# Half of the low halves of a kernel's last weights made by an adding DMA in the place of a VectorE subtraction

## The chip, the cores and the metric

The kernel runs on 1 core of one Trainium2 chip. The metric is device time in microseconds (us), the median of several runs. Before the change it is 1040.36 us, median of 3 runs (1040.05 to 1041.47).

## The reference, cut to what matters

Three transformer blocks follow one another over 256 tokens of 1024 features: a forgetting attention with a SwiGLU feed-forward, a retention with a SwiGLU feed-forward and a last norm, and a hybrid of differential and sparse attention with a gated feed-forward. All is float32. The part that the change reaches is the last block:

```
h = rms_norm(x, attn_pre_norm)
mix = hybrid_mixer(h, ...)            # projections, two kinds of heads, concat @ w_out
x = x + rms_norm(mix, attn_post_norm)
h = rms_norm(x, ffn_pre_norm)
f = (silu(h @ w_gate) * (h @ w_up)) @ w_down      # w_gate, w_up: 1024 x 2816; w_down: 2816 x 1024
x = x + rms_norm(f, ffn_post_norm)
```

## The kernel before, in words

Every product with a weight matrix is made in three matmuls of a reduced-precision float type (fp32r): each operand is split in a high half, the operand rounded to fp32r, and a low half, the operand minus its high half; high x high, high x low and low x high are summed in PSUM (mm3, L228 to L230; mm_wide at L243 and L244 does the same in two matmuls with both halves of the activations side by side).

The weights are read once, in granules of 128 x 1024 floats, 512 KB (some are smaller). The plan of all granules is a list in the order of use, 342 long. `gran` makes one: SP loads it into one of 4 raw buffers (L218), ACT copies it to wh, rounding it (L221), and DVE subtracts wh from raw into wl (L222). wh and wl have 6 buffers each. `take` hands the next granule to a caller and makes those ahead, up to 6 from the one that is taken, so that a granule's buffers are filled again as soon as PE is done with the granule 6 before it. `self.made` counts the granules made.

The order of the instructions on each engine is set by a scheduler when the program is built, from the order of the code and its own costs; each engine then runs its queue in order.

The last block: the hybrid's projections and heads, from some 735 us on. While the heads run (DVE and ACT do the softmax, the sparse heads first and then the differential ones), PE fills in with the projection of the differential heads from hyb_w (12 granules, `parts`) and then with w_out (8 granules). diff_norm squares the heads' outputs on ACT (don, da), POOL raises to -1/2 (dr), DVE scales (don). The handover follows: post_prep squares the sum on ACT (sq), POOL makes the reciprocal root (nr, L325), DVE updates x (xg) and scales it (pg), PE turns it (tr), and ACT and DVE split it again (xt, L249 and L250), for the first 128 tokens and then for the others. The last feed-forward (ffn with out set) takes 8 granules of 2 x 512 columns for gate and up of the first 512 columns (xs: all four gate granules for the first token tile, then for the second), then 36 granules of gate and up in pairs (ws_wide), the dense stretch, and 22 rows of w_down (out_proj), of which the last four are used bank after bank at the end.

Of the kernel before, what the change touches and what calls it, by code (L numbers as in the profile page):

```python
# [10 lines left out]
F32 = mybir.dt.float32  # L11
F32R = mybir.dt.float32r
AF = mybir.ActivationFunctionType
OP = mybir.AluOpType
# [124 lines left out]
class Net:  # L139
    def __init__(self, ctx, tc, ins):  # L140
        self.ctx, self.tc, self.nc = ctx, tc, tc.nc
        self.ins = ins
        self.c0, self.c1, self.c2 = (ins[f"const_{i}"] for i in range(3))
        nc = self.nc
        P = lambda name, bufs, **kw: ctx.enter_context(tc.tile_pool(name=name, bufs=bufs, **kw))
        self.cst = P("cst", 1)
        self.wp = P("wp", 1)
        self.sm = P("sm", 4)
        self.scr = P("scr", 2)
        self.ps = P("ps", 1, space=PSUM)  # L150
        cst = self.cst
        c0 = cst.tile([128, 808], F32, name="c0")
        self.c0t = c0
        self.ident = c0[:, 0:128]
        self.upper = c0[:, 128:256]
        self.ones = c0[:, 256:384]
        self.mask3 = c0[:, 384:768]
        self.sum8 = c0[0:16, 768:776]
        self.sum32 = c0[0:64, 776:808]
        self.xg = cst.tile([128, 48 + 8 * S], F32, name="xg")  # L160
        self.gT = self.xg[:, 0:48].rearrange("p (i k) -> p i k", i=6)
        self.XR = self.xg[:, 48:48 + 8 * S].rearrange("p (k s) -> p k s", k=8)
        self.gfg = cst.tile([128, 8], F32, name="gfg")
        self.XT = cst.tile([128, 8, 2, S], F32R, name="xt")
        self.XH, self.XL = self.XT[:, :, 0, :], self.XT[:, :, 1, :]
        self.mhalf = cst.tile([128, 8], F32, name="mhalf")
        nc.gpsimd.memset(self.mhalf, -0.5)
        self.r = [None, None]
        self.scale = None
        self.squares = []  # L170
        self.queue, self.ready, self.taken, self.made = [], [], 0, 0

    def phase_pool(self, ctx, name):
# [40 lines left out]
    def gran(self, src, nk):  # L214
        nc = self.nc
        n = src.shape[-1]
        w = self.wp.tile([128, n], F32, name="raw", tag="raw", bufs=4)
        nc.sync.dma_start(w, src)  # L218
        H = self.wp.tile([128, n], F32R, name="wh", tag="wh", bufs=WBUFS)
        L = self.wp.tile([128, n], F32R, name="wl", tag="wl", bufs=WBUFS)  # L220
        nc.scalar.activation(H, w, AF.Copy)  # L221
        nc.vector.tensor_sub(L, w, H.bitcast(F32))  # L222
        cut = lambda a: a.rearrange("p (k n) -> p k n", k=nk)
        return cut(H), cut(L)

# [660 lines left out]
    def hybrid(self, gp, gn):  # L886
        nc = self.nc
        ins = self.ins
        TT, STT = nc.vector.tensor_tensor, nc.vector.scalar_tensor_tensor
        with ExitStack() as st:  # L890
# [274 lines left out]
            def out_tiles(i):  # L1165
                OH[i] = p.tile([128, 4, S], F32R, name=f"oh{i}", tag="oT", bufs=4)
                OL[i] = p.tile([128, 4, S], F32R, name=f"ol{i}", tag="oT", bufs=4)
# [3 lines left out]
            def d_evac(i, t, ps):  # L1171
# [6 lines left out]
                else:  # L1178
                    a = p.tile([128, 512], F32, name=f"dv{t}")
                    nc.scalar.activation(a, ps, AF.Copy, scale=rr[t])  # L1180
                    dv.append(a)

            out_tiles(1)
            parts = []
            for i in range(3):
# [215 lines left out]
```

## Time and profile before

| | |
|---|---|
| median of 3 runs | 1040.36 us (1040.05 to 1041.47) |
| the profiled execution | 1041.37 us |
| its span, first to last instruction | 1039.6 us |
| PE, PEld busy | 98%, 84% of the span |
| DVE, ACT, POOL busy | 71%, 55%, 2% |
| mean granted TensorE clock | 0.996 |
| bytes moved | 181.18 MB, mean 174 GB/s |

The profile is of one execution. PE is the matmul engine and PEld its weight load, DVE is VectorE, ACT ScalarE, POOL GpSimd, SP the engine that issues the loads. Busy times of pipelined matmuls overlap, so a busy PE isn't PE at its peak; a wait in brackets behind a row is idle time of that engine just before it, with what ended it. The granted clock is a share of 2.4 GHz. Line numbers (L222) are those of the kernel before.

### The profile page before, as it was taken

What the parts mean: (1) busy time and instruction counts of PE and PEld (TensorE: products, weight loads), DVE (VectorE), ACT (ScalarE), POOL (GpSimd) and SP (SyncE); (2) the same over time, 40 slices, a digit from 0 to 9 for tenths busy, and PEclk for the clock granted to TensorE, in tenths of its full rate; (3) what the DMA queues carried; (4) which work ended last, traced back from release to release, by engine and by line L of the source; (5) the groups of instructions that cost most, each with busy time, mean ns of one, the idle gap of its engine ahead of it and who ended that gap; (6) DMA issues with size and microseconds to landing.
All of it is one profiled execution on the core that took longest, in us unless ns stands there. A gap on an engine that the chain in (4) does not pass through costs nothing.

```text
span 1039.6 us, 15367 instructions
## 1 busy us (share of the span) xinstructions
PE 1022.5 (98%) x5798; PEld 876.8 (84%) x5798; DVE 733.0 (71%) x1243; ACT 568.6 (55%) x914; POOL 19.8 (2%) x30
## 2 busy tenths in 40 slices
PE   7999999999999999999999999999999989999997
PEld 6999888888889889888888888888787668888885
DVE  6855977766777766767777777778887676776643
ACT  6545665665453353355565655556656665566532
POOL 1000000000000000000000000000000010000000
PEclk9999999999999999999999999999989999999999
DMA  8643666556665456456666666655633146566651
GB/s 267 217 146 118 234 184 197 183 179 185 188 201 173 151 162 183 141 171 195 215 211 186 182 188 186 184 174 175 210 104 120 31 154 202 193 183 191 192 172 40
DMA packets 53384, 181.18 MB, mean 174 GB/s; under 512 B 6832, under 2 KB 8368, under 8 KB 53184
## 3 DMA queue, kind: packets, MB, share of 16 engines
q1 hardware_dynamic: 53280, 180.19, 55.5%
q8 instruction: 45, 0.74, 0.3%
q14 instruction: 27, 0.22, 0.1%
q0 software_dynamic: 32, 0.03, 0.0%
HBM read 179.15 MB, written 1.05 MB: 173 GB/s over the span
## 4 chain that ended last, share of the span: by engine, by line
PE 95%; DVE 2%; DMA 1%; ACT 1%; issue 1%; POOL 0%; DVEq 0%; ACTq 0%; POOLq 0%
PE acc L243 23%; PE acc L244 12%; PE s L243 11%; PE acc L228 11%; PE acc L230 11%; PE acc L229 11%; PE s L244 6%; PE o L1154 1%; DVE wl L222 1%; PE o L228 1%; PE o L230 1%; PE o L229 1%; DMA raw<-in_hyb_w_dram 0%; DMA raw<-in_v_w_dram 0%; PE tr L845 0%
## 5 line engine op out<-in xcount | busy, mean ns | idle before, releaser
L222 DVE TENSOR_TENSOR wl<-raw,wh 128x1024 fp32r<-128x1024 f32 (+2 forms) x342 | 406.8, 1192 | 206.7 <-ACT wh L221 206.1
L221 ACT ACTIVATE wh<-raw 128x1024 fp32r<-128x1024 f32 (+2 forms) x342 | 352.7, 1033 | 278.4 <-PE acc L230 64.5
L243 PE MATMUL acc<-xt,wh 128*128 128x512 f32 x496 | 180.7, 397 | 0.0
L243 PE MATMUL s<-xt,wh 128*128 128x512 f32 x496 | 180.6, 397 | 0.0
L244 PE MATMUL acc<-xt,wl 128*128 128x256 f32 x496 | 129.5, 281 | 0.0
L244 PE MATMUL s<-xt,wl 128*128 128x256 f32 x496 | 129.3, 281 | 0.0
L243 PE MATMUL acc<-ht,wh 128*128 128x512 f32 x352 | 122.1, 392 | 0.0
L228 PE MATMUL acc<-wh,xt 128*128 128x512 f32 (+1 forms) x288 | 116.5, 405 | 1.9 <-ACT xt L249 1.8
L230 PE MATMUL acc<-wh,xt 128*128 128x512 f32 (+1 forms) x288 | 114.9, 399 | 1.2 <-DVE xt L250 1.2
L229 PE MATMUL acc<-wl,xt 128*128 128x512 f32 (+1 forms) x288 | 114.4, 397 | 0.0
L243 PEld LDWEIGHTS acc<-xt,wh 128*128 128x128 f32 x496 | 93.3, 188 | 16.8
L243 PEld LDWEIGHTS s<-xt,wh 128*128 128x128 f32 x496 | 93.3, 188 | 16.8
L244 PEld LDWEIGHTS s<-xt,wl 128*128 128x128 f32 x496 | 93.6, 189 | 5.9
L244 PEld LDWEIGHTS acc<-xt,wl 128*128 128x128 f32 x496 | 93.7, 189 | 5.6
L244 PE MATMUL acc<-ht,wl 128*128 128x256 f32 x352 | 96.6, 282 | 0.0
L243 PEld LDWEIGHTS acc<-ht,wh 128*128 128x128 f32 x352 | 65.1, 188 | 13.4
L228 PE MATMUL acc<-xt,wh 128*128 128x256 f32 x256 | 73.2, 286 | 0.0
L230 PE MATMUL acc<-xt,wl 128*128 128x256 f32 x256 | 72.1, 282 | 0.0
L229 PE MATMUL acc<-xt,wh 128*128 128x256 f32 x256 | 72.1, 281 | 0.0
L244 PEld LDWEIGHTS acc<-ht,wl 128*128 128x128 f32 x352 | 66.3, 188 | 1.5
L228 PEld LDWEIGHTS acc<-wh,xt 128*128 128x128 f32 x288 | 55.0, 191 | 14.6 <-ACT xt L249 2.2
L230 PEld LDWEIGHTS acc<-wh,xt 128*128 128x128 f32 x288 | 55.2, 192 | 13.4 <-DVE xt L250 1.6
(350 smaller groups left out, 1510.5 us busy)
## 6 DMA issues: line engine op xcount, KB each, us to landing
raw<-in_ffn_w_dram SPq DMA_DIRECT2D x132, 512.0 KB, 3.7
raw<-in_ret_w_dram SPq DMA_DIRECT2D x48, 512.0 KB, 3.5
raw<-in_ffn_out_dram SPq DMA_DIRECT2D x32, 512.0 KB, 3.7
raw<-in_w_down_dram SPq DMA_DIRECT2D x22, 512.0 KB, 3.6
raw<-in_fox_w_dram SPq DMA_DIRECT2D x20, 512.0 KB, 4.6
raw<-in_hyb_w_dram SPq DMA_DIRECT2D x20, 512.0 KB, 4.1
raw<-in_ret_out_dram SPq DMA_DIRECT2D x16, 512.0 KB, 3.9
raw<-in_ffn_out_dram SPq DMA_DIRECT2D x16, 384.0 KB, 3.5
```

The lines of the kernel that those rows point to most:

```text
L221: nc.scalar.activation(H, w, AF.Copy)
L222: nc.vector.tensor_sub(L, w, H.bitcast(F32))
L228: mm(out, xh, wh, start=first, stop=False, **kw)
L229: mm(out, xh, wl, start=False, stop=False, **kw)
L230: self.last = mm(out, xl, wh, start=False, stop=last, **kw).ins
L243: whole = lambda: mm(ps, H, x, start=first, stop=last).ins
L244: part = lambda: mm(ps[:, 0, :], L, x[:, 0, :], start=False, stop=False).ins
L1154: nc.tensor.matmul(o[hs, t, :], VN[i // 2][:, i % 2, g, :], pt[:, 2 * t + i, :], start=i == 0, stop=i == n - 1)
```

## The change

A flag is set where the hybrid's sparse heads begin. From there on, each granule with an odd number gets its low half in another way: ACT writes the negated high half into wl, and POOL issues a DMA that reads the weights a second time from DRAM and adds them to wl.

```
         H = self.wp.tile([128, n], F32R, name="wh", tag="wh", bufs=WBUFS)
         L = self.wp.tile([128, n], F32R, name="wl", tag="wl", bufs=WBUFS)
         nc.scalar.activation(H, w, AF.Copy)
-        nc.vector.tensor_sub(L, w, H.bitcast(F32))
+        if self.dma_low and self.made % 2:
+            nc.scalar.activation(L, H.bitcast(F32), AF.Copy, scale=-1.0)
+            nc.gpsimd.dma_start(L, src, accum_op=OP.add)
+        else:
+            nc.vector.tensor_sub(L, w, H.bitcast(F32))
...
+            self.dma_low = True
             out_tiles(1)
             parts = []
```

In __init__ the flag is set to False, which moves the lines behind it by one; behind gran they are moved by five and behind the flag by six, so L222 of before is L227 of the change, and its negating copy and DMA are L224 and L225.

The order of the instructions changes with it, from the stretch of the heads on. POOL, from the middle of the program to its end, before (nr are reciprocal roots of norms, xc a buffer that is cleared):

```order
L338 TENSOR_TENSOR nr_5093<-nv,mhalf 128x2
L979 MEMSET xc 128x512 x2
L338 TENSOR_TENSOR nr_6915<-nv,mhalf 128x2
L338 TENSOR_TENSOR nr_6924<-nw,mhalf 128x2
L1243 TENSOR_TENSOR dr<-da,mhalf 128x4 x2
L325 TENSOR_TENSOR nr<-nv,mhalf 128x1 x6
```

And in the change, from the heads on:

```order
L225 DMA wl<-in_hyb_w_dram 128x1024 x4
L225 DMA wl<-in_w_out_dram 128x1024 x3
L1249 TENSOR_TENSOR dr<-da,mhalf 128x4 x2
L225 DMA wl<-in_w_out_dram 128x1024
L225 DMA wl<-in_ffn_w_dram 128x1024
L330 TENSOR_TENSOR nr<-nv,mhalf 128x1 x2
L225 DMA wl<-in_ffn_w_dram 128x1024
L330 TENSOR_TENSOR nr<-nv,mhalf 128x1
L225 DMA wl<-in_ffn_w_dram 128x1024
L330 TENSOR_TENSOR nr<-nv,mhalf 128x1
L225 DMA wl<-in_ffn_w_dram 128x1024 x19
L225 DMA wl<-in_w_down_dram 128x1024 x11
```

The DMAs stand between the small operations of the norms, 41 in all.

DVE at the end of the heads, before (da and don are diff_norm's, ol the low half of its result):

```order
L250 TENSOR_TENSOR ol_8100<-tr,oh_8099 128x512
L222 TENSOR_TENSOR wl<-raw,wh 128x1024 x3
L1241 TENSOR_SCALAR da<-da 128x4
L1245 SCALAR_TENSOR_TENSOR don<-o,dr,subln 128x128 x4
L222 TENSOR_TENSOR wl<-raw,wh 128x1024
```

And in the change:

```order
L255 TENSOR_TENSOR ol_8106<-tr,oh_8105 128x512
L227 TENSOR_TENSOR wl<-raw,wh 128x1024
L1247 TENSOR_SCALAR da<-da 128x4
L1251 SCALAR_TENSOR_TENSOR don<-o,dr,subln 128x128 x4
L227 TENSOR_TENSOR wl<-raw,wh 128x1024
```

Three subtractions ahead of the second da have become one.

DVE a little later, at the end of the handover's first token tile, before (xg and pg are post_prep's, xt the low half of what PE multiplies next):

```order
L495 TENSOR_TENSOR pg<-acc,gain 128x512
L513 SCALAR_TENSOR_TENSOR xg<-pg,nr,xg 128x4x128 x2
L514 TENSOR_TENSOR pg<-xg,gain 128x512 x2
L222 TENSOR_TENSOR wl<-raw,wh 128x1024 x2
L250 TENSOR_TENSOR xt<-tr,xt 128x4x128 x2
```

And in the change (nv takes ACT's squares of x, nf takes POOL's nr):

```order
L500 TENSOR_TENSOR pg<-acc,gain 128x512
L518 SCALAR_TENSOR_TENSOR xg<-pg,nr,xg 128x4x128 x2
L519 TENSOR_TENSOR pg<-xg,gain 128x512 x2
L227 TENSOR_TENSOR wl<-raw,wh 128x1024
L328 SCALAR_TENSOR_TENSOR nv<-na 128x1
L493 TENSOR_SCALAR nf<-nr 128x1
L255 TENSOR_TENSOR xt<-tr,xt 128x4x128 x2
```

One of the two subtractions ahead of xt is gone, and nv and nf have moved in front of xt.

ACT in the handover, from the first token tile's xt to the second's, before (sq are the squares for the norms, sg the gate's activation):

```order
L249 ACTIVATE xt<-tr 128x4x128 x2
L318 ACTIVATE sq,na<-xg 128x512
L221 ACTIVATE wh<-raw 128x1024
L318 ACTIVATE sq,na<-acc 128x512
L221 ACTIVATE wh<-raw 128x1024
L318 ACTIVATE sq,na<-s 128x512
L318 ACTIVATE sq,na<-xg 128x512 x2
L611 ACT_TABLE_LOAD
L611 ACTIVATE sg<-acc,nr 128x512
L249 ACTIVATE xt<-tr 128x4x128 x2
```

And in the change:

```order
L254 ACTIVATE xt<-tr 128x4x128 x2
L323 ACTIVATE sq,na<-acc 128x512
L224 ACTIVATE wl<-wh 128x1024
L323 ACTIVATE sq,na<-s 128x512
L222 ACTIVATE wh<-raw 128x1024 x2
L224 ACTIVATE wl<-wh 128x1024
L323 ACTIVATE sq,na<-xg 128x512 x2
L616 ACT_TABLE_LOAD
L616 ACTIVATE sg<-acc,nr 128x512
L254 ACTIVATE xt<-tr 128x4x128 x2
```

Negated copies (L224) have come in between the squares, and two wh copies and one negated copy stand ahead of the second pair of sq<-xg.

PE between the two groups of 16 matmuls of 16 columns, which make the compressed scores, before (the last two of the first group and the first of the second):

```order
L1081 MATMUL o<-KCH,QS_7168 128x16
L1082 MATMUL o<-KCL,QS_7168 128x16
L1121 MATMUL s<-KTH,QS_7168 128x256
L1122 MATMUL s<-KTL,QS_7168 128x256
L229 MATMUL acc<-wl,xt 128x512
L230 MATMUL acc<-wh,xt 128x512
L228 MATMUL acc<-wh,xt 128x512
L1081 MATMUL o<-KCH,QS_7169 128x16
```

And in the change:

```order
L1086 MATMUL o<-KCH,QS_7168 128x16
L1087 MATMUL o<-KCL,QS_7168 128x16
L234 MATMUL acc<-wl,xt 128x512
L235 MATMUL acc<-wh,xt 128x512
L233 MATMUL acc<-wh,xt 128x512
L234 MATMUL acc<-wl,xt 128x512
L1086 MATMUL o<-KCH,QS_7169 128x16
```

The two scores matmuls of 256 columns have moved ahead of the first group, and one matmul of 512 columns more stands between the groups.

## Rows read from the trace of the kernel before

**Rows 1.** The page: busy us by engine (share of span), and chain by engine.
```profile
PE 1022.5 (98%) x5798; PEld 876.8 (84%) x5798; DVE 733.0 (71%) x1243; ACT 568.6 (55%) x914; POOL 19.8 (2%) x30
...
PE 95%; DVE 2%; DMA 1%; ACT 1%; issue 1%; POOL 0%; DVEq 0%; ACTq 0%; POOLq 0%
```

**Rows 2.** Timeline of PE, 820 to 853: start, us, [idle before].
```profile
831.86 0.50 PE L1251 MATMUL tr<-c,don 128*128 128x128 f32 x2 [0.60 <-DVE don L1245]
...
843.99 0.50 PE L230 MATMUL acc<-wh,xt 128*128 128x512 f32 x1 [1.21 <-DVE xt L250]
...
848.06 0.39 PE L229 MATMUL acc<-wl,xt 128*128 128x512 f32 x1
...
852.00 0.50 PE L228 MATMUL acc<-wh,xt 128*128 128x512 f32 x1 [1.54 <-ACT xt L249]
```

**Rows 3.** Windows: length, each engine's busy us; last clock, DMA share, GB/s.
```profile
880.00:970.00 90.00, 90.00 (x512) 78.30 (x512) 65.00 (x88) 54.68 (x80) 0.00 (x0) 1.00 0.60 187
...
730.00:740.00 10.00, 9.25 (x49) 6.97 (x47) 9.27 (x15) 6.69 (x8) 0.00 (x0) 1.00 0.82 277
728.00:729.00 1.00, 1.00 (x6) 0.82 (x5) 0.10 (x2) 0.87 (x1) 0.00 (x0) 1.00 0.98 401
```

**Rows 4.** Groups of instructions by line, 760 to 1040: busy, mean ns.
```profile
L222 DVE TENSOR_TENSOR wl<-raw,wh 128x1024 fp32r<-128x1024 f32 x77 | 93.8, 1223 | 57.4 <-ACT wh L221 57.3
L221 ACT ACTIVATE wh<-raw 128x1024 fp32r<-128x1024 f32 x76 | 80.2, 1057 | 55.8 <-PE o L230 26.2 <-PE s L243 17.0 <-PE acc L230 9.0
```

**Rows 5.** Timeline of ACT in the dense stretch, 919 to 932.
```profile
919.61 1.06 ACT L221 ACTIVATE wh<-raw 128x1024 fp32r<-128x1024 f32 x1 [0.95 <-PE s L243]
921.10 0.39 ACT L637 ACTIVATE sg<-s 128x256 f32<-128x256 f32 x1 [0.42 <-PE s L243]
921.38 1.05 ACT L221 ACTIVATE wh<-raw 128x1024 fp32r<-128x1024 f32 x1
...
925.26 1.06 ACT L221 ACTIVATE wh<-raw 128x1024 fp32r<-128x1024 f32 x1 [0.95 <-PE s L243]
```

**Rows 6.** DMA issues: count, KB each, us to landing; POOL's issue in ns.
```profile
raw<-in_ffn_w_dram SPq DMA_DIRECT2D x132, 512.0 KB, 3.7
...
f<-in_fox_f_dram POOLq DMA_DIRECT2D x1, 32.0 KB, 3.6
...
L549 POOL DMA_DIRECT2D f<-in_fox_f_dram x1: 708/708/708, 1.3 to 1.3; - x1
```

**Rows 7.** Timeline of SP from 850, and of DVE and PE near the end.
```profile
850.95 96.11 SPq L218 DMA_DIRECT2D raw<-in_ffn_w_dram  x35
950.19 57.87 SPq L218 DMA_DIRECT2D raw<-in_w_down_dram  x22
...
1017.63 1.23 DVE L222 TENSOR_TENSOR wl<-raw,wh 128x1024 fp32r<-128x1024 f32 x1 [1.56 <-ACT wh L221]
...
1024.24 0.40 PE L229 MATMUL acc<-wl,ht 128*128 128x512 f32 x1
```

**Rows 8.** Timeline of DVE, then POOL, in the handover.
```profile
826.48 3.68 DVE L222 TENSOR_TENSOR wl<-raw,wh 128x1024 fp32r<-128x1024 f32 x3 [0.26 <-ACT wh L221]
...
840.98 2.36 DVE L222 TENSOR_TENSOR wl<-raw,wh 128x1024 fp32r<-128x1024 f32 x2
...
844.68 1.46 POOL L325 TENSOR_TENSOR nr<-nv,mhalf 128x1 f32<-128x1 f32 x1 [6.27 <-DVE nv L323]
```

**Rows 9.** Timeline of ACT in the handover.
```profile
843.95 0.59 ACT L318 ACTIVATE sq<-acc 128x512 f32<-128x512 f32 x1
...
847.91 0.63 ACT L318 ACTIVATE sq<-xg 128x512 f32<-128x512 f32 x1 [1.76 <-DVE xg L513]
```

**Rows 10.** Windows of a microsecond where the granted clock falls (columns as in rows 3).
```profile
758.00:759.00 1.00, 1.00 (x10) 1.00 (x9) 0.00 (x0) 0.00 (x0) 0.00 (x0) 0.76 0.83 229
759.00:760.00 1.00, 1.00 (x4) 0.90 (x5) 0.63 (x3) 0.00 (x0) 0.00 (x0) 0.50 0.66 172
...
765.00:766.00 1.00, 1.00 (x8) 0.81 (x7) 0.00 (x0) 0.20 (x1) 0.00 (x0) 0.83 0.06 16
```

More of the change, by code (lines that the diff above doesn't have):

```diff
@@ L170, in __init__ @@
         self.squares = []
+        self.dma_low = False
         self.queue, self.ready, self.taken, self.made = [], [], 0, 0
```

## The prediction

> **What bounds the kernel now.** I read the page's busy table and its chain first: PE is busy 1022.5 of 1039.6 us, DVE 733.0, and 95% of the chain that ended last is PE [rows 1]. So work that moves between DVE, ACT and the DMA engines gains only where PE is seen to wait, and loses wherever an operand of PE comes late. Then the PE timeline of the stretch in which the change begins: its three longest waits stand in the handover from the hybrid to the last feed-forward, 0.60, 1.21 and 1.54 us [rows 2], each behind a chain through DVE, ACT and POOL; from there to the end PE has no idle time of note. Then the windows of the dense stretch: in 880 to 970 PE is busy 90.00 of 90 us, ACT 54.68, and the 16 DMA engines have a share of 0.60 at 187 GB/s [rows 3]. The profiled execution took 1041.37 us for a span of 1039.6 and lies 1.0 above the median of the three runs, 1040.36; I sum against it and take the 1.0 off at the end. About 0.2%, 2.1 us, is what a measurement of this kernel can tell from no change.
>
> **The parts.** The order of POOL lists 41 adding DMAs, 4 + 4 for the hybrid, 22 for gate and up, 11 for down, so the change does what it says and no rival is needed for that.
>
> *DVE* loses 41 subtractions of 1223 ns [rows 4], 50 us. In the dense stretch PE doesn't wait for DVE, so this is worth nothing there; its cover is the lead of six buffers.
>
> *ACT* gains 41 copies of the shape of the wh copy, 1057 ns [rows 4], 43 us. In the dense stretch that is one per pair of granules. A pair lasts 5.65 us (919.61 to 925.26 [rows 5]), so 16 copies add 17 us to 54.68 of 90 and ACT stays below full. The lead holds too: PE ends a pair at about 921.1, ACT makes the second granule's high half from 921.38 [rows 5] and the negated one until about 923.5. PE wants that buffer two pairs and a quarter later, at 921.1 + 11.3 + 1.4 = 933.8. The add has some 10 us from issue to use.
>
> *POOL* issues the adds. The one DMA it issued before, of 128 rows, took 708 ns of it and 3.6 us to landing [rows 6]. 41 of these make 29 us on an engine with nothing else to do in the dense stretch. The nr pows stand behind an issue in POOL's queue, but each such issue follows a copy that ACT makes ahead of the sq that feeds the pow, so it has 0.6 us of sq as cover: nothing, or a tenth or two if the cover goes.
>
> *The adding DMA* has no row. Per granule it moves 512 KB, and it must read its destination beside its source. Below, it costs the DMA engines one plain pass; above, three (two reads and a write in turn). I take two, because a plain pass holds one read and this one holds two. A pass takes 512 KB over the rate of full queues. The rows give 187 GB/s at share 0.60, 277 at 0.82 and 401 at 0.98 [rows 3], which is 312, 338 and 409 per full share: queues that are fuller move more per busy time, so I take the last, 1.31 us a pass; the second gives 1.55. From 850.95 on SP still issues 35 + 22 = 57 plain loads [rows 7], and 30 adds fall in the same time, 117 passes. At 1.31 us they end 153 us later, at 1004; at 1.55, at 1032. Before, the last low half was ready at 1017.63 + 1.23 = 1018.9, and PE first used it at 1024.24 [rows 7]. So by my value the adds are hidden: 0 us. At 1.55 they cost 1032 - 1024 = 8. The Trainium skill (Collectives: The Full Stack, the section on the bandwidth ceiling) says that a DMA that adds emits two read descriptors per chunk on the same ring and so delivers about half the rate of a copy, 32.35 against 62.28 GB/s; by it the sum would be the one above, with two passes, and no row here shows it. It speaks against the change.
>
> *The handover* is the place where I expect a visible difference. A gain: DVE did three subtractions (826.48, 3.68 us) ahead of the second da [rows 8]; now one stands there, and ACT makes the don squares after two wh copies instead of three, so da comes some 1 us earlier and the wait of 0.60 goes, -0.6. No gain: two subtractions at 840.98 held DVE's xt up [rows 8] and one is left, 1.2 us less, but in the new order nv and nf of the first token tile stand ahead of xt too, and nf waits for POOL's nr, which took 1.46 us here [rows 8]. With wl until 842.2, nv, and nr until 843.9, the first half of xt is ready near 844.6, where it let PE go at 843.99 [rows 2]: +0.7, with the gain +0.1. A cost: the fourth granule of gate (the second of the feed-forward that is added) gets its negated half on ACT behind both xt and the first sq of the second token tile. That sq ran at 843.95 [rows 9] for 0.6, so the copy ends near 845.6, and 0.6 earlier with the gain ahead of it, 845.0. A plain load of 512 KB lands 3.7 us after its issue [rows 6], here at 848.7, and with a second pass of 1.31 at 850.0. PE reached this granule's low half at 848.06 [rows 2], now at 848.2: a new wait of 0.5 to 1.8 us. Behind it ACT does two wh and one negated copy, 3.2 us, ahead of the next sq, in the place of one wh and 1.76 us of idle time [rows 9], some 1.3 us later; but the xt that PE waits for at 852.00 also stands behind the gate's sg, which waits for the same late accumulator, so the two delays run side by side and are not summed. The handover gives +0.6 to +1.9; bounds -1.8, if both waits ahead go, and +1.9. I take +1.0, what the plain landing gives and a third of the second pass.
>
> *The clock.* From 758 to 766 PE ran at a granted clock of 0.50, which is 1.2 GHz of 2.4, after 32 matmuls of 16 columns. The loss is 0.24 + 6 x 0.50 + 0.17 = 3.4 us (six full microseconds at 0.50, their neighbours at 0.76 and 0.83 [rows 10]). The new order keeps both groups of 16 with four wide matmuls between them, so I take 0; bounds -3.4 and +3.4 (a second fall).
>
> Sum: 1041.4 + 0 + 1.0 + 0 - 1.0 = about 1041, no change that can be told.
>
> **The rivals.**
>
> *The DMA engines become the bound.* If the queues can't go past the rate of the ten-microsecond window, the adds pile up in the dense stretch and PE waits for wl a little in every pair. It decides from the point at which 57 loads and 30 adds need more than 1024 - 851 = 173 us, a pass of 1.48 us at two passes per add. At 1.55 us it costs 8 us; by the share of the dense stretch itself (0.60 of 5.65 us for two granules, 1.70 a pass) 117 passes end at 1050, +26. Between them +14: 1055 (1046 to 1067). For it: no ten-microsecond window moves more than 277 GB/s [rows 3]. Against: the last row of [rows 3], and 10 us of lead. The Trainium skill (DMA: Bandwidth & Descriptors, Issuing engines are not separate DMA queues) says that DMAs from POOL run on the same 16 engines as those from SP and interleave with them; by that rule the second queue brings no rate of its own, as this rival has it.
>
> *Three passes or more.* 147 passes end at 850.95 + 193 = 1044 or, at 1.55 us, 1079: +20 to +55, some 1080. Nothing in the rows speaks for it but that no row excludes it.
>
> *Faster.* The fourth granule's add is in time and POOL's nr is over before DVE comes to nf, so that the waits of 0.60 and 1.21 go, -1.8; or the clock no longer falls, -3.4; or both, -5.2: about 1037.5, between 1035 and 1038.5. For it: DVE was the engine ahead of two of the three waits. Against: ACT takes what DVE gives, in the same chain.
>
> **How the numbers follow.** Hidden with a handover that is about even: 0.46, 1041 (1038 to 1045, mostly inside the 2.1 us). DMA-bound: 0.28. Three passes: 0.11. Faster: 0.15. Faster by over 0.2% takes 0.14 from the last and 0.09 from the first: 0.23. Slower takes 0.28, 0.11 and 0.10 from the first: 0.49. The rest, 0.28, is no change. The single likeliest case is no change, though the slower ones together hold more; its own range is 1038 to 1045. The range of 8 in 10 goes from 1036 to 1066 and leaves out the third case and the outer ends of the DMA-bound and the faster one.
>
> **What would show it.** In the changed profile the dense stretch should read 280 GB/s or more with PE at 90.00 of 90, ACT near 72, and no PE wait with wl's DMA as releaser; the DMA share tells how many passes an add has (0.9 is one, near 1.0 with a landing of 6 to 8 us is two). At the handover a wait of 0.5 to 2 us on the add of a gate granule, and none of 0.60 ahead of the second don. I am wrong if PE waits for wl in most pairs from 880 on (the first rival), if landings exceed 10 us (the second), or if the clock's fall near 760 is gone (the third).

## The result and the profile after

| | before | after |
|---|---|---|
| median | 1040.36 us (1040.05 to 1041.47) | 1048.2 us (1045.28 to 1050.95, 5 runs) |
| the profiled execution | 1041.37 us | 1046.59 us |
| its span | 1039.6 us | 1044.8 us |
| last matmul's end to the end of the span | 6.4 us | 6.9 us |
| mean granted TensorE clock | 0.996 | 0.996 |

The change is slower: the ratio is 1.0074, with a 95% interval from 1.0062 to 1.0085, or 7.8 us. The profiled execution is one of the shorter; in the three runs above 1048 us the mean granted clock is 0.991 or 0.992 where it is 0.996 here, and 0.004 to 0.005 of 1047 us is 4 to 5 us.

The page of the changed kernel, busy time by engine, the two DMA queues (packets, MB, share of 16 engines), and the chain by engine; the first and last of these lines answer to [rows 1]:

```profile
PE 1023.1 (98%) x5798; PEld 876.5 (84%) x5798; DVE 687.3 (66%) x1202; ACT 606.8 (58%) x955; POOL 53.2 (5%) x71
...
q1 hardware_dynamic: 53280, 180.19, 53.3%
q0 software_dynamic: 5936, 21.53, 11.5%
...
PE 92%; DMA 3%; DVE 2%; issue 1%; ACT 1%; POOL 0%; DVEq 0%; ACTq 0%; POOLq 0%
```

DVE is 45.7 us less busy and ACT 38.2 us more, and a second queue moves 21.5 MB, as the change says. What is new is DMA in the chain. The dense stretch, as in [rows 3], the windows of the changed kernel:

```profile
880.00:970.00 90.00, 90.00 (x513) 78.30 (x512) 47.19 (x73) 67.90 (x96) 13.63 (x16) 1.00 1.02 281
```

PE is busy 90.00 of 90 us as before, while the DMA share rose from 0.60 to 1.02 and the rate from 187 to 281 GB/s. So the loss isn't there. The waits of PE from 734 us on, changed kernel (us in total, times, longest):

```profile
PE acc L234 <- DMA wl<-in_ffn_w_dram: 3.3, 1, 3.3
PE acc L234 <- DMA wl<-in_w_out_dram: 2.3, 1, 2.3
PE acc L234 <- DMA wl<-in_hyb_w_dram: 1.5, 1, 1.5
PE acc L233 <- ACT xt L254: 1.4, 2, 1.1
PE acc L233 <- DVE rm L933: 0.4, 1, 0.4
PE tr L1257 <- DVE don L1251: 0.3, 1, 0.3
```

and the same view of the kernel before:

```profile
PE acc L228 <- ACT xt L249: 1.8, 2, 1.5
PE acc L230 <- DVE xt L250: 1.2, 1, 1.2
PE tr L1251 <- DVE don L1245: 1.2, 2, 0.6
PE tr L965 <- DVE nat L930: 0.6, 2, 0.4
```

The handover's waits, 4.2 us before (1.8 + 1.2 + 1.2), are 1.7 now (1.4 + 0.3), so 2.5 us are gained; three waits for an adding DMA, one each, cost 7.1. That is +4.6 of the 5.2 us between the two spans; 0.5 is the longer tail behind the last matmul. The three in the timeline of PE, each a matmul with the low half of an added granule:

```profile
751.59 0.51 PE L234 MATMUL acc<-wl,xt 128*128 128x512 f32 x1 [1.54 <-DMA wl<-in_hyb_w_dram]
...
833.66 0.50 PE L234 MATMUL acc<-wl,oh 128*128 128x512 f32 x1 [2.26 <-DMA wl<-in_w_out_dram]
...
851.11 0.67 PE L234 MATMUL acc<-wl,xt 128*128 128x512 f32 x1 [3.28 <-DMA wl<-in_ffn_w_dram]
```

The chain of the changed kernel (start, us, what) shows how long each add took from its issue to its landing:

```profile
742.68 8.87 DMA wl<-in_hyb_w_dram
...
827.67 5.95 DMA wl<-in_w_out_dram
...
845.12 5.95 DMA wl<-in_ffn_w_dram
```

By their place in the plan these are granules 261 (the first that is added), 275 (the last of w_out) and 279 (the fourth of gate and up, the one that the prediction looked at). PE wanted them at the start of its row less the wait in brackets, at 750.05, 831.40 and 847.83: they had a lead of 7.4, 3.7 and 2.7 us. In the dense stretch an add lands in 7.4 us (median), and PE waits for none there; the prediction's estimate of its lead was some 10 us.

The clock. The fall at 758 of [rows 10] isn't there in the changed kernel's profile, but two others are, right behind the two longer waits (windows, columns as in [rows 3]):

```profile
834.00:835.00 1.00, 1.00 (x4) 0.84 (x3) 0.00 (x0) 0.51 (x2) 0.00 (x0) 0.60 1.07 287
835.00:836.00 1.00, 1.00 (x4) 0.71 (x4) 0.69 (x1) 0.17 (x2) 0.00 (x0) 0.50 1.00 303
...
852.00:853.00 1.00, 1.00 (x4) 0.80 (x3) 0.00 (x0) 0.00 (x0) 0.00 (x0) 0.50 0.99 385
```

Each costs 1.7 us (for the first 0.40 + 0.50 + 0.50 + 0.31 in its four windows), together the 3.4 us of the fall before. In this one execution the clock therefore adds nothing.

### The profile page after: what moved, and what is told of

The parts are those of the page before. It is cut to its first block, busy times and chain, and to the rows that moved or that the text cites. A ratio compares the mean times of both kernels' runs of the same rounds, so it can differ in the third digit from the quotient of the medians.

```text
span 1044.8 us, 15432 instructions
## 1 busy us (share of the span) xinstructions
PE 1023.1 (98%) x5798; PEld 876.5 (84%) x5798; DVE 687.3 (66%) x1202; ACT 606.8 (58%) x955; POOL 53.2 (5%) x71
## 3 DMA queue, kind: packets, MB, share of 16 engines
HBM read 200.64 MB, written 1.05 MB: 193 GB/s over the span
## 4 chain that ended last, share of the span: by engine, by line
PE 92%; DMA 3%; DVE 2%; issue 1%; ACT 1%; POOL 0%; DVEq 0%; ACTq 0%; POOLq 0%
PE acc L248 23%; PE acc L249 12%; PE s L248 11%; PE acc L234 10%; PE acc L235 10%; PE acc L233 10%; PE s L249 6%; PE o L1159 1%; DMA wl<-in_hyb_w_dram 1%; DVE wl L227 1%; DMA wl<-in_w_out_dram 1%; DMA wl<-in_ffn_w_dram 1%; PE o L233 1%; PE o L235 1%; PE o L234 1%
## 5 line engine op out<-in xcount | busy, mean ns | idle before, releaser
L222 ACT ACTIVATE wh<-raw 128x1024 fp32r<-128x1024 f32 (+2 forms) x342 | 352.7, 1033 | 265.3 <-PE acc L235 65.2
L227 DVE TENSOR_TENSOR wl<-raw,wh 128x1024 fp32r<-128x1024 f32 (+3 forms) x301 | 357.2, 1188 | 216.5 <-ACT wh L222 215.6
L235 PE MATMUL acc<-wh,xt 128*128 128x512 f32 (+1 forms) x288 | 114.4, 398 | 0.0
L235 PE MATMUL acc<-xt,wl 128*128 128x256 f32 x256 | 72.1, 282 | 0.0
L234 PEld LDWEIGHTS acc<-wl,xt 128*128 128x128 f32 x288 | 54.9, 191 | 17.6 <-DMA wl<-in_ffn_w_dram 3.7
L233 PEld LDWEIGHTS acc<-wh,xt 128*128 128x128 f32 x288 | 54.9, 191 | 14.1 <-ACT xt L254 1.8
```

Of the source, the lines that this page charges most:

```text
L233: mm(out, xh, wh, start=first, stop=False, **kw)
L234: mm(out, xh, wl, start=False, stop=False, **kw)
L235: self.last = mm(out, xl, wh, start=False, stop=last, **kw).ins
```

## The experiments

Theory A: the adds are free wherever a granule is made with the full lead of six buffers; the loss is a few adds where the stages change, which land after PE wants them, and the clock that falls behind such waits. Theory B: the second read fills the DMA queues, and this costs in the dense stretch. Theory C: the cost is the new order in heads and handover with ACT's extra copies, not the DMA. All kernels are the changed one with another condition in gran; a granule that isn't added is subtracted on DVE. The ratios are to the kernel before as it was timed beside each group of runs: 1040.38, 1040.13 and 1040.37 us.

### The dense adds alone, and the early ones alone

```
-        if self.dma_low and self.made % 2:
+        if self.dma_low and self.made % 2 and self.made >= 284:
```

> The adds are left in only from granule 284 on, in the dense stretch (29 of 41); the heads and the handover subtract on VectorE as before. Theory A (the loss is three late adds at the changes of stage, and the clock that falls behind such waits; adds with the lead of six buffers are free): 1040.4 us, 1039.5 to 1042, with PE at 90.00 of 90 in 880 to 970, a DMA share near 1.0 there, no wait of PE on an add but some 0.3 us at the very end. Theory B (the second read fills the DMA queues and costs time in the dense stretch): most of the 7.8 us remain, 1045 to 1048. Theory C (the new order of the heads and ScalarE's extra copies there are the cost, not the adds themselves): about 1040, as A.

Measured: 1042.02 us, ratio 1.0015 [1.0006, 1.0023], 1.6 us. The window 880 to 970 has the change's traffic and no loss:

```profile
880.00:970.00 90.00, 90.00 (x512) 78.33 (x511) 47.54 (x72) 67.53 (x97) 13.76 (x16) 1.00 1.00 277
```

PE's waits in the handover are those of the kernel before and none is for an add; the last matmul ends at 1033.22 us, where before it ended at 1033.23. In this profile only the tail is 0.5 us longer. The other microsecond of the 1.6 isn't seen in it. The time lies at the upper edge of A's range, and C expected the same as A here: the run speaks against B alone.

```
-        if self.dma_low and self.made % 2:
+        if self.dma_low and self.made % 2 and self.made < 284:
```

> The adds are left in only up to granule 283 (12 of 41): hybrid, w_out and the first two of the feed-forward, and nothing in the dense stretch changes against the kernel before. Theory A: the whole loss, 1046 to 1049, with the same three waits of PE of about 1.5, 2.3 and 3.3 us and the granted clock falling to 0.50 behind at least one of them. Theory B: about 1040 to 1042, since the dense stretch has its old traffic of 187 GB/s. Theory C: the whole loss, as A.

Measured: 1047.8 us, ratio 1.008 [1.0068, 1.0093], 7.4 us: nearly the whole loss from 12 adds of 41, with no added traffic in the dense stretch. So B falls. The waits of PE:

```profile
PE acc L234 <- DMA wl<-in_w_out_dram: 3.2, 1, 3.2
PE acc L234 <- DMA wl<-in_ffn_w_dram: 2.8, 1, 2.8
PE acc L233 <- ACT xt L254: 1.7, 2, 0.9
```

The same two late adds; the first, of hyb_w, wasn't waited for. Behind the second the clock was below full from 848 to 859, nine whole microseconds of it at 0.50.

### Without the three that PE waited for

```
-        if self.dma_low and self.made % 2:
+        if self.dma_low and self.made % 2 and self.made not in (261, 275, 279):
```

> Three adds of 41 are taken out, those PE waited for: the first (granule 261, hyb_w), the one that stood behind the second dr on GpSimd (275, w_out) and the second of the feed-forward (279); VectorE subtracts there. Theory A: the waits of 1.5, 2.3 and 3.3 us go, 7.1 us, and the handover stays 2.5 us shorter than before: 1037 to 1041, with no wait on an add above 0.5 us, unless the next add in line (263 or 277) is then late itself, which would give 1040 to 1043. Theory B: 1045 or more, since 38 of 41 adds are still there. Theory C: 1044 to 1048, since nearly all of ScalarE's copies and of the new order stay.

Measured: 1043.88 us, ratio 1.003 [1.0018, 1.0042]. The waits on adds are gone, and the time is 4.3 us below the change's, but it is above A's range, and above the 1040 to 1043 for another late add. A new wait stands behind the handover (timeline of PE, then the DVE row it waits for, with the one ahead of it):

```profile
870.29 0.86 PE L623 MATMUL tr<-c,sg 128*128 128x128 f32 x4 [2.66 <-DVE sg L620]
```

```profile
868.40 1.23 DVE L227 TENSOR_TENSOR wl<-raw,wh 128x1024 fp32r<-128x1024 f32 x1 [6.70 <-ACT wh L222]
869.55 1.28 DVE L620 TENSOR_TENSOR sg<-acc,sg 128x512 f32<-128x512 f32 x2
```

The gate's product sg stands behind a subtraction whose high half ACT makes late: by its row that copy waited for a matmul of PE (L235) and began at 867.32. I took this for the queues being full of adds; the last run below shows that this isn't enough. The wait isn't the whole either. In this profile the clock fell three times, near 758, at 843 and behind the wait at 870, and this cost 6.8 us where the kernel before lost 3.4 [rows 10]. A window of the second fall:

```profile
844.00:845.00 1.00, 1.00 (x4) 0.77 (x3) 0.95 (x2) 0.19 (x1) 0.50 (x1) 0.50 0.82 299
```

### What an add costs: two in a pair

```
-        if self.dma_low and self.made % 2:
+        if self.dma_low and self.made >= 284:
```

> Every granule from 284 on gets its low half by an add (58 adds, two per pair of granules in the place of one), none ahead of it; VectorE subtracts no weights there. This prices an add at the DMA engines: a pair lasts 5.65 us and now holds two plain loads and two adds. If an add costs what two plain passes cost (1.31 us each, six passes), a pair takes 7.9 us and the dense stretch and w_down grow by some 60 us, to 1100. If it costs 1.4 plain passes at the lower rate of the old dense stretch (1.70 us a pass), 8.2 us a pair, 1110. If it costs one pass at 1.31, 5.2 us a pair, still hidden: 1040 to 1045. Theory B would have any of the longer ones; theory A says nothing here but that one add per pair fits.

Measured: 1101.93 us, ratio 1.0596 [1.0576, 1.0615], where two passes per add were put at 1100. The two queues in 880 to 970 (packets, MB, share), and the two largest of PE's waits from 850 on:

```profile
q0 software_dynamic: 3386, 12.36, 68.7%
q1 hardware_dynamic: 3387, 12.34, 36.5%
```

```profile
PE acc L249 <- DMA wl<-in_ffn_w_dram: 23.4, 17, 2.9
PE acc L234 <- DMA wl<-in_w_down_dram: 15.2, 19, 1.5
```

Here the queues are the bound, and both carry the same bytes: an add takes 68.7 / 36.5 = 1.88 times the engines of a plain load. (In the dense stretch of the change the queues have 51.8% for 8.39 MB and 49.5% for 16.85 MB, which makes it 2.1.) 12.34 MB are 23.5 loads of 512 KB, and as many adds; 23.5 + 1.88 x 23.6 = 67.9 plain passes in 90 us are 1.33 us a pass. With one add per pair, 2 + 1.88 passes would take 5.15 of 5.65 us: by this estimate the change's dense stretch has half a microsecond per pair to spare, and a second add overruns it.

### ScalarE's copies without the DMA

```
-            nc.gpsimd.dma_start(L, src, accum_op=OP.add)
+            nc.vector.tensor_add(L, L.bitcast(F32), w)
```

> ScalarE writes the negated high half for all 41 granules as in the change, but VectorE adds the raw weights to it in the place of the DMA; no second read. It has the change's work on ScalarE, and none of its transfers. Theory A (the loss is the adding DMA that lands too late): no wait on a DMA of wl, 1040 to 1043, the handover's old waits of 0.6, 1.2 and 1.5 us there again and up to 1 us longer, since VectorE now waits for ScalarE's copy. Theory C (ScalarE's extra copies and the new order in heads and handover are the cost): 1045 to 1049.

Measured: 1043.22 us, ratio 1.0029 [1.0017, 1.004], just above A's range and well below C's. PE waits for no DMA, but new waits stand in the handover:

```profile
PE tr L527 <- DVE pg L519: 1.7, 1, 1.7
PE acc L233 <- ACT oh L254: 0.8, 1, 0.8
```

So the kernel with ACT's copies is some 3 us slower where DVE keeps its work and waits for them as well. That all of it is these waits isn't shown: in the profile, of the shortest of the ten runs, PE's waits sum to 1.5 us more than before, and the mean granted clock of the ten is 0.9943 against 0.9974, which alone would be 3 us. The copies aren't a cost as such: the last run holds 37 of these 41 and is faster than the kernel before.

### Only adds that came in time, and the two late ones alone

```
+        if self.dma_low and self.made in (263, 265, 267, 269, 271, 273, 277):
```

> Seven adds are left, those that came in time: granules 263 to 273 with odd numbers, and 277. Theory A: the run without three adds lost 2.66 us at 870 because the adds from 281 on filled the queues (share 1.01 in 860 to 866 against 0.89) while the weights of the dense stretch were to be loaded; without them this wait is gone, and the handover is 1 to 2 us shorter than in the kernel before (0.3 in the place of 0.6 ahead of don, none of 1.54 at 852): 1038 to 1040.5. If instead the handover ran too early for plain loads as well, the wait at 870 stays and the time is 1041 to 1044.

```
+        if self.dma_low and self.made in (275, 279):
```

> Two adds alone: granule 275 (the last of w_out) and 279 (the second added one of the feed-forward); the other 39 are subtracted on VectorE. Theory A: these two make most of the loss by themselves, waits of 2.3 to 3.3 us each, the gain of the handover (up to 2.5 us) smaller than in the change, and the clock falls behind a wait: 1044 to 1048. Theory B or C (it needs the other adds' traffic or ScalarE's other copies to make these late): below 1042.5.

```
+        if self.dma_low and self.made in (261, 263, 265, 267, 269, 271, 273, 277):
```

> The seven adds of the run before, and granule 261, the first of all: PE waited 1.54 us for it in the change and not at all in the run with the early adds alone. By theory A it costs the wait or nothing: the seven's time plus 0 to 1.5 us. The fall of the clock at 758 was missing in both kernels that hold this add; if that is owed to it, the time is the seven's less 3.4 us.

Measured: seven 1039.69 us, ratio 0.999 [0.9979, 1.0]; eight 1038.64 us, 0.9984 [0.9975, 0.9992], 1.5 us faster than the kernel before by the medians. The seven lie in A's range, with no wait near 870, but their interval reaches 1. When no add is late, the handover's waits are 1.8 us shorter than before, 2.4 for 4.2: the eight's waits of PE from 800 on are

```profile
PE acc L235 <- DVE xt L255: 1.3, 1, 1.3
PE acc L233 <- ACT xt L254: 0.8, 1, 0.8
PE tr L1257 <- DVE don L1251: 0.3, 1, 0.3
```

with none of the 1.54 of [rows 2], but with the 1.21 still there as 1.25. Granule 261 cost a wait of 1.86 in this profile, and the fall near 758 was missing. So in the profile the handover's 1.8 are used up by 261, and what it gains on the kernel before is the 3.4 us of that fall; how much of the 1.5 us between the medians is the handover isn't shown. The eight's time is 1.05 us less than the seven's, neither of the two values expected, and the two intervals overlap.

The two alone: 1044.43 us, ratio 1.0032 [1.0022, 1.0042]. The time is in A's range, but not by A's mechanism: PE waits for no add. It waits for ACT (oh, 1.41 us) and DVE (pg, 1.08; don, 0.76), which is nearer to what C says. On POOL the second dr was slow behind the issue of the add; beside it, DVE made a subtraction:

```profile
830.64 0.92 POOL L225 DMA_DIRECT2D wl<-in_w_out_dram  x1 [8.46 <-ACT wl L224]
831.29 2.14 POOL L1249 TENSOR_TENSOR dr<-da,mhalf 128x4 f32<-128x4 f32 x1
```

```profile
831.32 1.24 DVE L227 TENSOR_TENSOR wl<-raw,wh 128x1024 fp32r<-128x1024 f32 x1 [1.62 <-ACT wh L222]
```

It took 2.14 us here and 1.01 in the changed kernel, where no subtraction ran beside it. POOL's nr shows the same in the handovers of all these kernels: 0.54 to 0.57 us with no such subtraction beside it, 1.46 or 1.47 where one runs through it. So the subtraction, rather than the issue, is what goes with the slow dr. PE came to the added granules later behind their issue than in the change, and so they weren't late. Lateness is a difference, and both sides of it move.

### The four adds that were left, one by one

```
+        if self.dma_low and self.made in (261, 263, 265, 267, 269, 271, 273, 275, 277):
```

> The eight adds that were a little faster than the kernel before (1038.64 us), and granule 275, the last of w_out. With 279, 281 and 283 added too (the run of the twelve early adds) the time was 1047.8, so these four cost 9.2 us together. Theory A (lateness of the single add): a wait of PE of 2.3 to 3.2 us for it, and up to 1.7 us of lower clock behind the wait: 1041 to 1043.5. Theory D (no single add is late by itself; the order of ScalarE and GpSimd that the four bring about together costs): below 1040.

```
+        if self.dma_low and self.made in (261, 263, 265, 267, 269, 271, 273, 277, 279):
```

> The eight adds and granule 279, the second added one of the feed-forward. Theory A: a wait of PE of 2.8 to 3.3 us for it, and up to 1.7 us (in one run 5 us) of lower clock behind it: 1041.5 to 1045. Theory D: below 1040.

```
+        if self.dma_low and self.made in (261, 263, 265, 267, 269, 271, 273, 277, 281, 283):
```

> The eight adds, and 281 and 283, the next two of the feed-forward. Theory A: PE never waited for these, so 1038 to 1039.5. If the part of the 9.2 us that 275 and 279 don't show by themselves sits here (the adds delay the loads of the next granules, a wait near 870 as in the run without three), 1041 or more.

```
+        if self.dma_low and self.made % 2 and self.made not in (275, 279, 281, 283):
```

> 37 of 41 adds: all but 275, 279, 281 and 283. If the parts add up, the eight's 1038.64 plus the 1.6 us that the adds of the dense stretch cost by themselves: 1039.5 to 1041. If the dense adds delay the loads when the handover is shorter, the wait of 2.7 us near 870 of the run without three is there again: 1042 to 1044. Theory B (traffic): 1044 or more.

| | us | ratio to before | against the eight's 1038.64 |
|---|---|---|---|
| with 275 | 1044.09 | 1.0035 [1.0023, 1.0046] | +5.45 |
| with 279 | 1042.88 | 1.0025 [1.0013, 1.0037] | +4.24 |
| with 281 and 283 | 1040.19 | 0.9995 [0.9985, 1.0005] | +1.55 |
| 37 of 41 adds | 1039.04 | 0.9986 [0.9976, 0.9996] | +0.40 |

Of A's ranges for these only that of 279 was met (1041.5 to 1045): 275 is 0.6 us above its 1043.5, 281 and 283 are 0.7 above their 1039.5 and below the 1041 of the other case, and the 37 are half a microsecond faster than the parts added up. Each of the late ones brings its wait. With 275, the timeline of PE and the add in the chain:

```profile
836.73 0.80 PE L234 MATMUL acc<-wl,oh 128*128 128x512 f32 x1 [3.64 <-DMA wl<-in_w_out_dram]
```

```profile
829.35 7.33 DMA wl<-in_w_out_dram
```

With 279:

```profile
846.30 0.79 PE L234 MATMUL acc<-wl,xt 128*128 128x512 f32 x1 [2.62 <-DMA wl<-in_ffn_w_dram]
```

```profile
840.96 5.29 DMA wl<-in_ffn_w_dram
```

Their leads (row less wait, less issue) are 836.73 - 3.64 - 829.35 = 3.7 and 846.30 - 2.62 - 840.96 = 2.7 us, the same as in the change. The matmul behind the wait takes 0.79 or 0.80 us in the place of 0.50: the clock had fallen to 0.50 during it. With 281 and 283 there is a smaller wait, which I hadn't expected:

```profile
865.88 0.50 PE L234 MATMUL acc<-wl,xt 128*128 128x512 f32 x1 [1.33 <-DMA wl<-in_ffn_w_dram]
```

The last add ahead of it was issued at 856.08 us, 8.5 ahead of the want, landed after 9.8, and so was still late: a plain load issued at 858.01 took 8.01 us in the chain, and the queues had a share of 0.93 (850 to 860), refilling the buffers after the handover.

The 37 adds keep 90% of the change's second reads, with the dense stretch and w_down whole, and are 1.3 us faster than the kernel before. The four that are missing cost 1048.2 - 1039.04 = 9.2 us in the full change, and 1047.8 - 1038.64 = 9.2 in the run of the early adds: the same four, the same price, with and without the dense adds. One by one they make 5.45 + 4.24 + 1.55 = 11.2, so the parts don't simply add up. Some half of the price is the clock. The mean granted clock of the runs, on average, is 0.9934 in the change and 0.9973 with the 37 adds, 0.9924 with the early adds and 0.9976 with the eight; of some 1045 us that is an estimated 4.1 and 5.4 us. The waits for 275 and 279 in the change's profile are 5.5.

Theory A holds in the main: the loss is a few adds that come late where the stages change, and the lower clock that comes with them. Its list of three was wrong: 261 is waited for in the eight (1.86) and in the 37 (1.63), which are faster than the kernel before all the same, and 281 and 283 belong to the four, though their 1.55 us alone aren't clear of the two intervals. D, that no single add is late by itself, falls. In the run of the 37 the share in 860 to 870 is 0.99 and no wait near 870 is left, so full queues alone didn't make the one of the run without three.

## Why the prediction was right and wrong

**The DMA engines: right, in size too.** The step took two passes per add at 1.31 us (512 KB at the 401 GB/s of the row; at its own 409 per full share it would be 1.28). The run with two adds per pair gives 1.88 passes at 1.33 us. The Trainium skill (Collectives: The Full Stack, the section on the bandwidth ceiling) puts the add of a reduce-scatter at two reads on the same ring and gives a measured ratio of 1.93 to a copy; the 1.88 agrees. The Trainium skill's rule that DMAs of all issuing engines run on the same 16 DMA engines (DMA: Bandwidth & Descriptors, Issuing engines are not separate DMA queues) agrees as well: with both queues full their shares sum to 1.05, so the second brought no engines of its own. The DMA-bound rival named a pass of 1.48 us as the deciding point and took 1.55; the measured pass lies 0.15 us below the point.

**The dense stretch: right.** DVE's 41 subtractions brought nothing there, ACT's copies stayed hidden, with 67.90 of 90 us where I had added 17 to 54.68, and no pair waited. What the step left out is a tail 0.5 us longer.

**The handover: the place was right, the size of one term was not.** The fourth gate granule was to cost 0.5 to 1.8 us, and cost 3.28. The negated copy was to end at 845.0, and POOL issued the add at 845.12; PE was to want it at 848.2, and wanted it at 847.83. The mis-sized term is the landing: 3.7 us of a plain load up to 5.0 with a second pass, and measured 5.95. One plain pass more isn't all that an add has on a load. In 770 to 826 the queues of the changed kernel were quieter, with a share of 0.41, and its DMA issues there read (KB each, us to landing):

```profile
raw<-in_w_out_dram SPq DMA_DIRECT2D x4, 512.0 KB, 5.0
raw<-in_ffn_w_dram SPq DMA_DIRECT2D x4, 512.0 KB, 3.6
wl<-in_w_out_dram POOLq DMA_DIRECT2D x3, 512.0 KB, 5.7
```

That is 2.1 us above the quicker of the loads; a fourth add, of hyb_w, took 7.2. One of the three, issued at 804.98, had the queues to itself (all of the 144 packets from 804 to 812 are its own):

```profile
wl<-in_w_out_dram POOLq DMA_DIRECT2D x1, 512.0 KB, 5.6
```

So the longer landing isn't a matter of full queues alone. On top of it comes the burst of the handover: 0.97 of the engines were busy in 848 to 854.

**The step that failed is where it looked.** I worked out one granule of the handover and left the other added ones of hyb_w and w_out to the lead of six, though the cover was only shown for the dense stretch. Granule 275 had a lead of 3.7 us, because ACT made its negated half (826.30) behind the four squares of don, and because POOL's queue has the second dr ahead of the issue:

```profile
826.71 1.01 POOL L1249 TENSOR_TENSOR dr<-da,mhalf 128x4 f32<-128x4 f32 x1 [8.00 <-DVE da L1247]
827.67 0.89 POOL L225 DMA_DIRECT2D wl<-in_w_out_dram  x1
```

I had costed what the issues do to POOL's pows and not what a pow does to an issue. That wait, 2.26 us, and the 1.54 for granule 261 weren't in the sum.

**The gains: one right, one with the wrong sign.** The wait of 0.60 ahead of don at 831.86 is gone, as worked out; the 0.3 that is left is that of the first token tile, 0.59 before. The first xt was to come 0.7 us later, and came earlier: the wait of 1.21 is gone. DVE's nf did stand ahead of xt and did wait for POOL, but nr took 0.55 us there, where I had taken 1.46 from [rows 8]. That row had a subtraction of DVE beside it (844.51 to 845.73); in the new order DVE waits for nr, so that nothing runs beside it. Among the runs with adding DMAs the gain is there only where granules 277 and 279 are both added. In the eight and the 37 279 is subtracted, in the run of the two 277 is; a second subtraction stands ahead of xt again, and the wait is 1.23 to 1.25.

**The clock.** Zero, within 3.4 either way, was right for the profiled execution, but by luck: the fall that was to stay went, and two others of half its size came. It was too narrow for the median: in three of the five runs of the change the mean clock is 0.004 to 0.005 lower. The step looked at the matmuls of 16 columns and not at the new waits, behind which the clock falls.

The likeliest case, no change, was wrong, and the slower cases, which held more of the chance together, were slower for a reason that none of the rivals named: neither the bound nor three passes, but late single adds, of which the handover's step had one. That the wide range holds 1048.2 us is luck in so far: its upper part was there for the bound. The faster rival's sign, that the fall near 760 is gone, came true in a kernel that is slower. Its 1.8 us of the handover are there in number once the four late adds are taken out, but by other waits than it named: the 0.60 goes and the 1.21 stays, while 1.54 goes and 0.6 is new elsewhere; the medians are 1.5 us lower with the eight and 1.3 with the 37.

## What to carry to other kernels

A lead that is shown in the steady stretch says nothing of the changes of stage; for a transfer that takes longer than the instruction it replaces, work out issue, landing and want at each place where the engines' order changes, for every such transfer there. Here an adding DMA was cheap where its landing, mostly 6 to 8 us, fitted in the lead, and dear where the lead was 2.7 to 3.7 us; four of 41 turned a gain of 1.3 us into a loss of 7.8, some half of it by the clock that falls behind such waits. Choose by place rather than by every other one.

## What the runs showed of the hardware that I had not expected

An add of 512 KB from DRAM into SBUF landed 5.6 us after its issue with the queues to itself, where plain loads took 3.6 to 5.0; its issue holds POOL for 0.85 to 0.90 us. In full queues the two together moved 274 GB/s by destination bytes, where plain loads alone reached 401 for a microsecond [rows 3]. A small operation of POOL (nr) took 0.55 us alone and 1.46 beside a subtraction of DVE.

The same waits don't always bring the same clock. The seven and the eight have the same two waits at the start of the feed-forward, 0.84 and 1.23 against 0.83 and 1.25 us. In the seven the clock falls behind them (windows):

```profile
841.00:842.00 1.00, 0.66 (x2) 0.56 (x3) 1.00 (x3) 1.00 (x4) 0.00 (x0) 0.64 0.66 234
842.00:843.00 1.00, 1.00 (x4) 0.81 (x3) 1.00 (x3) 0.86 (x1) 0.37 (x1) 0.50 0.79 201
```

and in the eight it stays full:

```profile
842.00:843.00 1.00, 0.33 (x1) 0.30 (x2) 1.00 (x3) 1.00 (x2) 0.00 (x0) 1.00 0.80 328
843.00:844.00 1.00, 1.00 (x6) 0.80 (x5) 1.00 (x4) 1.00 (x3) 0.04 (x1) 1.00 0.56 164
```

In the same way the fall near 760 is there in the profiles of before, of the dense adds alone and of the seven, and missing in those of the change, the eight and the 37. I had thought that it might be owed to granule 261. All seven profiles of kernels that don't add 261 have the fall, and five of the seven that add it lack it; but two (with 275, and with 281 and 283) have it, so the add doesn't decide it alone. What does stays open, as does the rest of the 1.6 us that the dense adds cost by themselves and not on top of the eight. That an add could be issued earlier at these places (with a seventh buffer, or its negated half made ahead of the squares) wasn't tried.
